# The sigmoid gates of two branches, made at the end of each RWKV group instead of in their branch projections

## The chip, the core and the metric

The kernel runs on one core of a Trainium2 chip. The metric is device time in microseconds (us) of one execution. Engines are named as the profile names them: PE is TensorE's matmuls and PEld its weight loads, DVE is VectorE, ACT is ScalarE, POOL is GpSimd, SP issues most of the DMAs.

## The reference

One layer of a hybrid decoder on 256 tokens of 2048 channels, in float32. One input projection feeds three mixers (Mamba-2 SSD, RWKV-7, mLSTM) and three sigmoid gates; each mixer's output is projected, gated, and the sum goes through an output projection, a layer norm and a gated MLP. What matters here is the end of the token mixer:

```
proj = h @ w_in
(ssd_z, ssd_xbc, ssd_dt, rwkv_p, ml_qk, ml_v, ml_o, ml_i, ml_f, gate_pre) = split(proj)
y_ssd, y_rwkv, y_mlstm = ssd_mixer(...), rwkv7_mixer(...), mlstm_mixer(...)
g_ssd, g_rwkv, g_mlstm = split(sigmoid(gate_pre), 3)
merged = g_ssd * (y_ssd @ proj_ssd) + g_rwkv * (y_rwkv @ proj_rwkv) + g_mlstm * (y_mlstm @ proj_mlstm)
return merged @ w_out
```

A gate depends on `h` alone, not on its mixer.

## The kernel before

**Products.** Each weight matrix is read in blocks of 512 columns, 256 rows (a chunk) at a time: SP loads the chunk (`wraw`, 512 KB, four buffers), ACT rounds it to the fast matmul format (`whi`, L154), DVE subtracts to get the low half (`wlo`, L155), and TensorE adds three products, high by high, high by low and low by high. A product over 2048 rows has 8 chunks. `block_cm` gives a block with the channels on the partitions (192 matmuls with 256 columns, L167, L169, L171), `block_tm` one with the tokens on the partitions (96 matmuls with 512 columns, L185 to L187). The accumulators `acc` have four banks of PSUM, two products' worth.

**Stages.** Four RWKV groups of eight heads (`rwkv_group`), four SSD groups, the branch projections of RWKV and SSD, the mLSTM (`ml_in`, eight heads), its branch projection, the output projection, and the MLP.

**An RWKV group.** Three products r, k, v (channel-major), then a gate product. Then a chain of small work: the decay and the rates from small matmuls (L476) with scans; normalised keys (L503, L514); pairwise products of four chunks of 64 tokens (L551) with masks; an inversion of triangular blocks, on VectorE four transposes (L586), 31 dependent steps shared by VectorE and GpSimd (L601, L603) and more transposes (L610, L613); the recursion over the four chunks (L645 to L679), in which each step waits for the one before; the output with its gate and a layer norm (L694 to L723), stored to `ydram`.

**Gates.** `gate(i, j, page)` (L892) makes columns 512 j to 512 j + 511 of gate i by a `block_tm` product and a sigmoid into a page of on-chip memory. In `rwkv_group` the gate of the RWKV branch (i = 1) is made behind r, k and v and stored to the DRAM tile `gdram` over ACT's DMA queue (L466, L467). In `branch` (L899) that gate is loaded back over SP's queue (L905), while the gates of SSD (i = 0) and mLSTM (i = 2) are made there, one ahead of each of the four projection products (L907). VectorE multiplies the gate with the projection and GpSimd adds it to `merged` (L914, L915).

**Order.** The code is written in the order above, and a list scheduler lays it out on each engine: of the instructions that are ready in its own model of time, the one that stands first in the code goes first; loads and splits of weights go ahead of all. The order is fixed when the program is built, and each engine then works its list from first to last. Products that stand behind a chain in the code therefore fill the places where the chain waits. Work slots (`p0` to `p18` and others) are shared by tag, so a tile also waits until the last reader of its slot is done.

Of the kernel before, what the change touches and what calls it, by code (L numbers as in the profile page):

```python
# [9 lines left out]
F32 = mybir.dt.float32  # L10
# [4 lines left out]
PSUM = bass.MemoryType.PSUM  # L15
DRAM = bass.MemoryType.DRAM

P = 128
T = 256
# [6 lines left out]
ALPHA = float(2.0 ** 0.25)  # L26
# [21 lines left out]
# pages that hold the last weights of a product whose token tiles end one after the other  # L48
LATE = [("b4", "p18"), ("b0", "b1"), ("b2", "b3"), ("p0", "p1"), ("p2", "p15"), ("p4", "p5")]

# columns of the one per-channel array: constants first, then vectors of the inputs
# [39 lines left out]
class Pair:  # L91
    """A channel-major operand split in two, as tiles of `n` row blocks each."""
# [11 lines left out]
class Layer:  # L104
# [11 lines left out]
    def pg(self, tag, shape, name, dtype=F32):  # L116
        """A tile in one of the shared work slots: p0..p17, b0..b4, s0..s3."""
        return self.wp.tile(shape, dtype, name=name, tag=tag)
# [14 lines left out]
    # ---------------------------------------------------------------- weights  # L133
    def chunks(self, W, nkt, pieces, pages=()):
        """hi and lo of row block after row block; the last chunks in the given pages."""
        nc, tc = self.nc, self.tc
        width = max(o + n for o, _, n in pieces)
        for c in range(0, nkt, KC):
            n = min(KC, nkt - c)
            self.nchunk += 1  # L140
            with tc.high_priority() if self.nchunk > 3 else nullcontext():
                raw = self.sp.tile([P, KC, 512], F32, name="wraw", bufs=4)
                for o, c0, w in pieces:
                    nc.sync.dma_start(
                        out=raw[:, :n, o:o + w],
                        in_=W[c * P:(c + n) * P, c0:c0 + w].rearrange("(k p) n -> p k n", p=P))
                i = c // KC - ((nkt + KC - 1) // KC - len(pages))
                if i < 0:
                    hi = self.sp.tile([P, KC, 512], F32R, name="whi")
                    lo = self.sp.tile([P, KC, 512], F32R, name="wlo", bufs=3)  # L150
                else:
                    hi, lo = [self.pg(t, [P, KC, 512], "wlate", F32R) for t in pages[i]]
                r = raw[:, :n, :width]
                nc.scalar.copy(out=hi[:, :n, :width], in_=r)  # L154
                nc.vector.tensor_tensor(out=lo[:, :n, :width], in0=r,  # L155
                                        in1=hi[:, :n, :width].bitcast(F32), op=ALU.subtract)
            for k in range(n):
                yield c + k, hi[:, k], lo[:, k]
# [19 lines left out]
    def block_tm(self, W, c0, X, nkt=KT, pages=()):  # L178
        """With pages the second token tile ends later, after all of the first."""
        nc = self.nc  # L180
        acc = [self.psA.tile([P, 512], F32, name="acc") for _ in range(2)]

        def mm(tt, kt, wh, wl):
            s = slice(tt * P, tt * P + P)
            nc.tensor.matmul(acc[tt], lhsT=X.h(kt)[:, s], rhs=wh, start=kt == 0, stop=False)  # L185
            nc.tensor.matmul(acc[tt], lhsT=X.h(kt)[:, s], rhs=wl, start=False, stop=False)  # L186
            nc.tensor.matmul(acc[tt], lhsT=X.l(kt)[:, s], rhs=wh, start=False, stop=kt == nkt - 1)  # L187

        late = []
        for kt, wh, wl in self.chunks(W, nkt, [(0, c0, 512)], pages):  # L190
            mm(0, kt, wh, wl)
            if kt // KC < (nkt + KC - 1) // KC - len(pages):
                mm(1, kt, wh, wl)
            else:
                late.append((kt, wh, wl))
        for w in late:
            mm(1, *w)
        return acc
# [6 lines left out]
    # ------------------------------------------------------------- layer norm  # L205
    def to_cm(self, n, gname, bname, X):
        """token-major normalised n -> X = g*n+b channel-major, split in two."""
        nc = self.nc
        hi, lo = X.hi[0], X.lo[0]
        for kt in range(0, KT, 2):  # L210
            ps = self.bank().rearrange("p (a t) -> p a t", a=2)
            for a in range(2):
                for tt in range(2):
                    c = (kt + a) % 4 * P
                    nc.tensor.transpose(out=ps[:, a, tt * P:(tt + 1) * P],  # L215
                                        in_=n(tt, (kt + a) // 4)[:, c:c + P], identity=self.c("ident"))
            tmp = self.pg("s%d" % (kt // 2 % 2), [P, 2, T], "tocm")
            for a in range(2):
                g, b = self.v(gname, kt + a), self.v(bname, kt + a)
                nc.scalar.activation(out=hi[:, kt + a], in_=ps[:, a], func=AF.Identity, scale=g, bias=b)  # L220
                nc.vector.tensor_scalar(out=tmp[:, a], in0=ps[:, a], scalar1=g, scalar2=b,
                                        op0=ALU.mult, op1=ALU.add)
            nc.vector.tensor_tensor(out=lo[:, kt:kt + 2], in0=tmp,
                                    in1=hi[:, kt:kt + 2].bitcast(F32), op=ALU.subtract)

    def moments(self, st, tt, act=False):
        """1/std, -mean/std and mean from the statistics of 4 column blocks."""
        nc, cp = self.nc, self.cp
        mv = cp.tile([P, 2], F32, name="mv", bufs=2)
        rstd = cp.tile([P, 1], F32, name="rstd", bufs=2)  # L230
# [15 lines left out]
    def normalise(self, blk, st):  # L246
        """blk(tt, j) <- (blk - mean) * rstd; one token tile on each of two engines."""
        nc = self.nc
        m = [self.moments(st, tt) for tt in range(2)]
        for j in range(NB):  # L250
            t = blk(0, j)
            nc.scalar.activation(out=t, in_=t, func=AF.Identity, scale=m[0][0], bias=m[0][1])
            t = blk(1, j)
            nc.vector.tensor_scalar(out=t, in0=t, scalar1=m[1][2], scalar2=m[1][0],
                                    op0=ALU.subtract, op1=ALU.mult)

    def affine_tm(self, r, name):
        """r <- r * g + b, token-major."""
        nc = self.nc
# [9 lines left out]
    def residual_tm(self, W, Y, nkt, r, st, before=None):  # L269
        """r <- ALPHA*r + Y^T W, with statistics per 512 columns."""  # L270
# [10 lines left out]
    # ---------------------------------------------------------------- evacuation  # L281
# [18 lines left out]
    # ---------------------------------------------------------------- prologue  # L300
    def prologue(self):
# [28 lines left out]
        # derived small vectors  # L330
# [7 lines left out]
    def smalls(self):  # L338
        """LoRA inputs, SSD time steps, mLSTM gates."""
# [16 lines left out]
        # softplus / log-sigmoid: i,f on partitions 64..79, dt on 96..127  # L356
# [22 lines left out]
        # q = atanh(s) = log1p(exp(-|x|)) / 2  # L379
# [8 lines left out]
        # SSD: local cumulative sums of a*dt  # L388
# [21 lines left out]
        # mLSTM: stabiliser  # L410
# [28 lines left out]
    # ---------------------------------------------------------------- RWKV-7  # L439
# [6 lines left out]
    def rwkv_group(self, g):  # L446
# [19 lines left out]
        gate = self.gate(1, g, 18)  # L466
        nc.scalar.dma_start(out=self.gdram[:, g], in_=gate)  # L467
# [12 lines left out]
        # decay: cumulative sums within chunks, then P and 1/P  # L480
# [16 lines left out]
        # normalised keys (negated)  # L497
# [20 lines left out]
        # kh = k (1 + (a-1) k_a)  # L518
# [5 lines left out]
        # av <- -(kk a)  # L524
        gps.tensor_tensor(out=av, in0=av, in1=nk, op=ALU.mult)
        # bonus
# [5 lines left out]
        # operands and pairwise products, chunk after chunk  # L532
# [30 lines left out]
        # token-major values  # L563
# [16 lines left out]
        # inverse of the unit triangular matrices: 32x32 diagonal blocks by substitution  # L580
# [54 lines left out]
        # chunks in order; rows: even heads R | Y, odd heads Y | R  # L635
# [44 lines left out]
        # output gate  # L680
# [16 lines left out]
        # per-head layer norm  # L697
# [27 lines left out]
    # ---------------------------------------------------------------- SSD  # L725
# [11 lines left out]
    def ssd_group(self, g, Y):  # L737
# [12 lines left out]
        # scores [s, l]: columns (s0,l0) (s0,l1) (s1,l1)  # L750
# [58 lines left out]
    # ---------------------------------------------------------------- mLSTM  # L809
# [34 lines left out]
    def ml_head(self, h, q, k, Y):  # L844
# [6 lines left out]
        # exponent: min(g[s] - c[l], mask)  # L851
# [39 lines left out]
    # ---------------------------------------------------------------- branches  # L891
# [6 lines left out]

    def branch(self, i, name, Y, merged, last=None):  # L899
        nc, a = self.nc, self.a  # L900
        vec, gps = nc.vector, nc.gpsimd
        for j in range(NB):
            if i == 1:
                g = self.pg("p%d" % (4 + j % 2), [P, 2, 512], "gate")
                nc.sync.dma_start(out=g, in_=self.gdram[:, j])  # L905
            else:
                g = self.gate(i, j, 4 + j % 2)  # L907
# [14 lines left out]
    def transposed(self, src, c0):  # L922
        """Two column tiles of token-major src(tt, c), channel-major in a PSUM bank."""
# [7 lines left out]
    def split_scaled(self, ps, w, hi, lo):  # L931
        """hi + lo = ps * w for one column tile in PSUM."""
# [8 lines left out]
    def run(self, upto=None):  # L941
# [3 lines left out]
        self.gdram = self.dp.tile([P, 4, 2, 512], F32, name="gdram")  # L945
# [100 lines left out]
def pack(i):  # L1046
    """Lays the inputs out for the kernel: weights as they are, per-channel vectors as columns."""
# [47 lines left out]
```

## Time and profile before

Three runs: 2489.68, 2487.14 and 2489.25 us, median 2489.25. The profiled execution has no time of its own beside its span of 2489.2 us, from the first to the last instruction, which lies between the runs.

| stretch of the span (us) | what runs | PE busy | DVE busy | POOL busy | granted clock |
|---|---|---|---|---|---|
| 0 to 118.7 | layer norm, first products | 101.7 | 80.0 | 5.6 | 1.00 |
| 118.7 to 773.4 | RWKV groups to the end of the last recursion | 606.0 | 567.1 | 333.7 | 0.97 |
| 773.4 to 902.5 | rest of SSD | 126.7 | 103.7 | 55.3 | 1.00 |
| 902.5 to 1173.3 | branches of RWKV and SSD, with 4 gates | 270.8 | 142.9 | 26.9 | 1.00 |
| 1173.3 to 1459.0 | mLSTM | 285.7 | 179.6 | 15.1 | 1.00 |
| 1459.0 to 1641.0 | branch of mLSTM, with 4 gates | 181.9 | 96.5 | 21.8 | 1.00 |
| 1641.0 to 1731.0 | output projection | 90.0 | 51.6 | 3.5 | 1.00 |
| 1731.0 to 2489.2 | layer norm, MLP, layer norm | 737.1 | 460.5 | 55.7 | 0.99, then 0.97 |

The columns are the time within the stretch in which the engine had an instruction under way, and the mean share of its clock that TensorE was granted. Matmuls overlap in their pipeline, so that PE can be busy without a gap and yet start matmuls at less than its full rate; the number of matmuls in a stretch shows that.

### The profile page before, as it was taken

The numbers are of one execution on the slowest core, as the hardware profiler recorded it, in microseconds if no ns is written. First come the engines' busy times: TensorE is split into PE (matmuls) and PEld (weight loads), VectorE is DVE, ScalarE is ACT, GpSimd is POOL, SyncE is SP. The second block draws the span as 40 slices with busy tenths as digits, with TensorE's granted clock in tenths as the row PEclk, the third lists the DMA queues.
The fourth block names the chain that finished last, engine by engine and source line by source line (L and its number), as shares of the span: only waits on it lengthen the run. The fifth ranks groups of instructions, "written<-read, shape, count | busy, mean of one in ns | idle before, by whom it ended". The sixth has DMA issues, their size and how long they took to land.

```text
span 2489.2 us, 41687 instructions
## 1 busy us (share of the span) xinstructions
PE 2399.9 (96%) x16602; PEld 2152.9 (86%) x16602; DVE 1681.8 (68%) x2116; ACT 1249.3 (50%) x1634; POOL 517.7 (21%) x488
## 2 busy tenths in 40 slices
PE   7999898989999999999999999999999999999997
PEld 7988787877989988888988888887999999997886
DVE  6678988897997875544666665456766666664445
ACT  4555455444646654443456654444554555453333
POOL 0046463564643520001000022000200000000000
PEclk9999999999999999999999999999999999999999
DMA  7654434244445656655655566555556556556554
GB/s 237 187 161 133 127 102 151 85 136 140 133 140 170 193 185 206 208 190 191 186 179 175 181 204 213 186 190 185 180 184 185 186 186 187 186 177 215 193 191 148
DMA packets 280276, 435.09 MB, mean 175 GB/s; under 512 B 25432, under 2 KB 118032, under 8 KB 279696
## 3 DMA queue, kind: packets, MB, share of 16 engines
q1 hardware_dynamic: 278640, 427.70, 54.4%
q8 instruction: 130, 2.13, 0.3%
q10 hardware_dynamic: 864, 2.62, 0.3%
q0 software_dynamic: 576, 2.10, 0.2%
q14 instruction: 66, 0.54, 0.1%
HBM read 423.90 MB, written 8.43 MB: 174 GB/s over the span
## 4 chain that ended last, share of the span: by engine, by line
PE 81%; DVE 11%; issue 3%; POOL 2%; ACT 2%; DMA 1%; SPq 0%; DVEq 0%; POOLq 0%; ACTq 0%
PE acc L186 13%; PE acc L187 13%; PE acc L185 13%; PE acc L171 12%; PE acc L169 12%; PE acc L167 12%; DVE wlo L155 4%; DVE si L603 1%; PE mix L551 1%; DVE si L601 1%; DVE xt L613 1%; DMA wraw<-in_w_in 1%; DVE ni L586 1%; ACT whi L154 1%; PE mix L788 1%
## 5 line engine op out<-in xcount | busy, mean ns | idle before, releaser
L155 DVE TENSOR_TENSOR wlo<-wraw,whi 128x1024 fp32r<-128x1024 f32 (+2 forms) x756 | 986.0, 1307 | 672.0 <-ACT whi L154 664.3
L154 ACT CAST whi<-wraw 128x1024 fp32r<-128x1024 f32 (+2 forms) x756 | 786.6, 1042 | 854.5 <-PE acc L187 446.0
L171 PE MATMUL acc<-xh,wlo 128*128 128x256 f32 x3104 | 887.2, 286 | 27.8 <-DVE wlo L155 27.5
L167 PE MATMUL acc<-xh,whi 128*128 128x256 f32 x3104 | 884.6, 285 | 3.0 <-ACT whi L154 2.7
L169 PE MATMUL acc<-xl,whi 128*128 128x256 f32 x3104 | 884.4, 285 | 0.0
L171 PEld LDWEIGHTS acc<-xh,wlo 128*128 128x128 f32 x3104 | 590.8, 191 | 36.8 <-DVE wlo L155 32.7
L167 PEld LDWEIGHTS acc<-xh,whi 128*128 128x128 f32 x3104 | 591.8, 191 | 8.2 <-ACT whi L154 3.1
L169 PEld LDWEIGHTS acc<-xl,whi 128*128 128x128 f32 x3104 | 591.1, 190 | 3.1 <-issue 1.0
L186 PE MATMUL acc<-wlo,xh 128*128 128x512 f32 x640 | 257.5, 402 | 9.2 <-DVE wlo L155 9.1
L187 PE MATMUL acc<-whi,xl 128*128 128x512 f32 x640 | 254.0, 397 | 0.0
L185 PE MATMUL acc<-whi,xh 128*128 128x512 f32 x640 | 233.9, 397 | 0.0
L186 PEld LDWEIGHTS acc<-wlo,xh 128*128 128x128 f32 x640 | 120.9, 189 | 38.7 <-DVE wlo L155 12.8
L185 PEld LDWEIGHTS acc<-whi,xh 128*128 128x128 f32 x640 | 120.9, 189 | 27.7
L187 PEld LDWEIGHTS acc<-whi,xl 128*128 128x128 f32 x640 | 121.0, 189 | 26.1
L186 PE MATMUL acc<-wlo,ah 128*128 128x512 f32 x322 | 126.9, 394 | 0.5 <-DVE wlo L155 0.5
L187 PE MATMUL acc<-whi,al 128*128 128x512 f32 x322 | 126.7, 393 | 0.0
L1006 POOL TENSOR_TENSOR fc<-fc 128x512 f32<-128x512 f32 (+1 forms) x22 | 28.7, 1303 | 447.2 <-DVE fc L293 440.3
L185 PE MATMUL acc<-whi,ah 128*128 128x512 f32 x322 | 113.4, 394 | 1.1 <-ACT whi L154 1.1
L915 POOL TENSOR_TENSOR merged<-merged,gate 128x512 f32<-128x512 f32 x16 | 28.2, 1788 | 342.8 <-DVE gate L914 342.8
L293 DVE SCALAR_TENSOR_TENSOR fc<-acc,fcols,fc 128x255 f32<-128x255 f32 (+1 forms) x172 | 77.0, 478 | 13.4 <-ACT fc L290 11.9
L266 POOL TENSOR_TENSOR res<-res,gb 128x1024 f32<-128x1024 f32 x16 | 43.7, 2730 | 203.3 <-PE mix L215 93.9
L603 POOL TENSOR_TENSOR yi<-yi,si 128x26 f32<-128x26 f32 (+12 forms) x104 | 73.3, 704 | 7.8
(360 smaller groups left out, 3134.2 us busy)
## 6 DMA issues: line engine op xcount, KB each, us to landing
wraw<-in_w_in SPq DMA_DIRECT2D x368, 512.0 KB, 3.4
wraw<-in_ffn_w_up SPq DMA_DIRECT2D x336, 256.0 KB, 3.1
wraw<-in_ffn_w_down SPq DMA_DIRECT2D x84, 512.0 KB, 4.4
wraw<-in_proj_rwkv SPq DMA_DIRECT2D x32, 512.0 KB, 4.5
wraw<-in_proj_ssd SPq DMA_DIRECT2D x32, 512.0 KB, 3.5
wraw<-in_proj_mlstm SPq DMA_DIRECT2D x32, 512.0 KB, 3.8
wraw<-in_w_out SPq DMA_DIRECT2D x32, 512.0 KB, 4.3
acb<-acd SPq DMA_DIRECT2D x16, 256.0 KB, 3.6
```

The costliest lines, as they stand in the source:

```text
L154: nc.scalar.copy(out=hi[:, :n, :width], in_=r)
L155: nc.vector.tensor_tensor(out=lo[:, :n, :width], in0=r, in1=hi[:, :n, :width].bitcast(F32), op=ALU.subtract)
L167: nc.tensor.matmul(a, lhsT=wh[:, o:o + m], rhs=X.h(kt), start=st, stop=False, skip_group_check=True)
L169: nc.tensor.matmul(a, lhsT=wh[:, o:o + m], rhs=X.l(kt), start=False, stop=False, skip_group_check=True)
L171: nc.tensor.matmul(a, lhsT=wl[:, o:o + m], rhs=X.h(kt), start=False, stop=kt == nkt - 1, skip_group_check=True)
L185: nc.tensor.matmul(acc[tt], lhsT=X.h(kt)[:, s], rhs=wh, start=kt == 0, stop=False)
L186: nc.tensor.matmul(acc[tt], lhsT=X.h(kt)[:, s], rhs=wl, start=False, stop=False)
L187: nc.tensor.matmul(acc[tt], lhsT=X.l(kt)[:, s], rhs=wh, start=False, stop=kt == nkt - 1)
L266: nc.gpsimd.tensor_tensor(out=r[j], in0=r[j], in1=gb[:, i].unsqueeze(1).to_broadcast([P, 2, 512]), op=op)
L293: nc.vector.scalar_tensor_tensor(out=dst[:, j:], in0=ps[:, :T - j], scalar=v(wname, (width - 1 - j) * nch + ct), in1=dst[:, j:], op0=ALU.m ...
L603: eng.tensor_tensor(out=t[:, j + 1:32, lo:e], in0=t[:, j + 1:32, lo:e], in1=tv, op=ALU.subtract)
L1006: nc.gpsimd.tensor_tensor(out=u, in0=u, in1=t[1][:, :n], op=ALU.mult)
```

## The change

The gates of SSD and mLSTM are made at the end of each RWKV group, behind its output in the code: for group g, block g of gate 0 and block g of gate 2, each stored to `gdram`, which grows from four to twelve blocks. `branch` loads every gate. The page p18 takes all of them in turn. The number of products, sigmoids and bytes of weights is the same; there are eight more stores and eight more loads of 512 KB. Comments are gone, which shifts some lines.

```
 (rwkv_group, behind v)
-        gate = self.gate(1, g, 18)
-        nc.scalar.dma_start(out=self.gdram[:, g], in_=gate)
+        self.spill_gate(1, g)
...
 (rwkv_group, end)
         nc.gpsimd.dma_start(out=self.ydram[:, 4 * g:4 * g + 4], in_=yo)

+        for i in (0, 2):
+            self.spill_gate(i, g)
...
+    def spill_gate(self, i, j):
+        self.nc.scalar.dma_start(out=self.gdram[:, i, j], in_=self.gate(i, j, 18))
+
     def branch(self, i, name, Y, merged, last=None):
         nc, a = self.nc, self.a
         vec, gps = nc.vector, nc.gpsimd
         for j in range(NB):
-            if i == 1:
-                g = self.pg("p%d" % (4 + j % 2), [P, 2, 512], "gate")
-                nc.sync.dma_start(out=g, in_=self.gdram[:, j])
-            else:
-                g = self.gate(i, j, 4 + j % 2)
+            g = self.pg("p%d" % (4 + j % 2), [P, 2, 512], "gate")
+            nc.sync.dma_start(out=g, in_=self.gdram[:, i, j])
             acc = self.block_tm(a[name], 512 * j, Y)
...
-        self.gdram = self.dp.tile([P, 4, 2, 512], F32, name="gdram")
+        self.gdram = self.dp.tile([P, 3, 4, 2, 512], F32, name="gdram")
```

The scheduler lays the whole RWKV stage out anew. The first place is VectorE in the recursion of group 1. `zm`, `zve` and `zvo` are the recursion's state; `nr`, `nrr`, `kh`, `nk`, `sq`, `l1e`, `l1o` and `bk` belong to the preparation and the pairwise products of group 2; `wlo` is the low half of a chunk of weights. Before:

```order
L155 TENSOR_TENSOR wlo<-wraw,whi 128x1024
L506 TENSOR_SCALAR nr<-nr 128x256
L669 COPY zm<-seq 128x256
L507 RECIPROCAL nr<-nr 128x256
L671 TENSOR_TENSOR zve<-zm,pl 64x4x64
L671 TENSOR_TENSOR zvo<-zm,pl 64x4x64
L155 TENSOR_TENSOR wlo<-wraw,whi 128x1024
L203 TENSOR_TENSOR nrr<-nr,nrr 128x256
L521 TENSOR_SCALAR kh<-av,cst,oka 128x256 x4
L155 TENSOR_TENSOR wlo<-wraw,whi 128x1024
L544 TENSOR_TENSOR l1e<-r,pext 64x4x64
L544 TENSOR_TENSOR l1o<-r,pext 64x4x64
```

The same place of the changed kernel (its lines L666, L668 and L670 are L667, L669 and L671 before; `v` is the evacuation of group 2's product v):

```order
L668 COPY zm<-seq 128x256
L670 TENSOR_TENSOR zve<-zm,pl 64x4x64
L670 TENSOR_TENSOR zvo<-zm,pl 64x4x64
L155 TENSOR_TENSOR wlo<-wraw,whi 128x1024 x2
L285 SCALAR_TENSOR_TENSOR v<-acc,cst,v 128x255
L155 TENSOR_TENSOR wlo<-wraw,whi 128x1024
L285 SCALAR_TENSOR_TENSOR v<-acc,cst,v 128x255 x2
L666 TENSOR_TENSOR zm<-zm,seq 128x256
L285 SCALAR_TENSOR_TENSOR v<-acc,cst,v 128x255
L670 TENSOR_TENSOR zve<-zm,pl 64x4x64
L670 TENSOR_TENSOR zvo<-zm,pl 64x4x64
L155 TENSOR_TENSOR wlo<-wraw,whi 128x1024 x5
```

Before, the preparation of group 2 stood between the steps of group 1's recursion; now weight splits and evacuations of products stand there, and the preparation comes behind the recursion.

The second place is TensorE where the mLSTM ends and its branch begins. `mn` is the output of the last head, transposed by L927 (L929 of the changed kernel), `acc_14479` the first gate of the branch, `acc_14628` its first projection product. Before:

```order
L927 MATMUL mix_14462<-cst_72,mn_14432 128x128
L185 MATMUL acc_14479<-whi_14609,xh_73 128x512
L186 MATMUL acc_14479<-wlo_14610,xh_73 128x512
L187 MATMUL acc_14479<-whi_14609,xl_74 128x512
L185 MATMUL acc_14480<-whi_14609,xh_73 128x512
L186 MATMUL acc_14480<-wlo_14610,xh_73 128x512
L187 MATMUL acc_14480<-whi_14609,xl_74 128x512
L185 MATMUL acc_14628<-whi_14632,ymh_11803 128x512
L185 MATMUL acc_14629<-whi_14632,ymh_11803 128x512
```

Now, where `acc_15093` and `acc_15094` are the first projection product and `acc_15259` and `acc_15260` the second; `ymh_12415` and `ymh_12416` are the first and the second half of the mLSTM's output:

```order
L929 MATMUL mix_15074<-cst_72,mn_15044 128x128 x3
L185 MATMUL acc_15259<-whi_15281,ymh_12415 128x512
L185 MATMUL acc_15260<-whi_15281,ymh_12415 128x512
...
L185 MATMUL acc_15259<-whi_15299,ymh_12415 128x512
L185 MATMUL acc_15260<-whi_15299,ymh_12415 128x512
L185 MATMUL acc_15093<-whi_15223,ymh_12416 128x512
L186 MATMUL acc_15093<-wlo_15224,ymh_12416 128x512
L185 MATMUL acc_15094<-whi_15223,ymh_12416 128x512
```

Before, a gate product filled the time up to the last transposes; now the first projection product is broken off ahead of its last chunk (`whi_15223`), which needs the last head, and the second one is drawn ahead.

## The prediction

> **What bounds the kernel now.** I read the page first (busy tenths over 40 slices, then the chain that ended last), then the busy time by stage, then the waits inside one RWKV group.
>
> ```profile
> PE   7999898989999999999999999999999999999997
> ...
> DVE  6678988897997875544666665456766666664445
> ...
> PE 81%; DVE 11%; issue 3%; POOL 2%; ACT 2%; DMA 1%; SPq 0%; DVEq 0%; POOLq 0%; ACTq 0%
> ```
>
> TensorE (PE) carries the chain; VectorE (DVE) has its 11% where its tenths reach 8 and 9, in slices 3 to 13, the RWKV groups. A slice is 62 us.
>
> ```profile
> core 0: us, PE busy (x) PEld busy (x) DVE busy (x) ACT busy (x) POOL busy (x), PEclk, DMA share, GB/s
> 425.80:581.50 155.70, 140.94 (x1304) 125.11 (x1296) 136.16 (x185) 80.14 (x126) 83.91 (x97) 0.98 0.39 123
> 1000.00:1050.00 50.00, 50.00 (x219) 40.78 (x218) 25.02 (x26) 23.54 (x25) 3.53 (x2) 1.00 0.62 205
> 1850.00:1900.00 50.00, 50.00 (x424) 50.00 (x423) 30.79 (x36) 24.46 (x30) 2.59 (x2) 1.00 0.61 184
> ```
>
> The last two rows give the price of a product at full rate. In the branch stage 219 matmuls of 128x512 start in 50 us, 0.228 us each, so a token-major product of 96 costs 21.9 us. In the FFN stage 424 of 128x256 start in 50 us, 0.118 us each, so a channel-major one of 192 costs 22.6 us. The first row is one RWKV group: it holds three channel-major products and one gate, 89.7 us at these prices, and takes 155.7 us.
>
> ```profile
> PEld acc L171 <- DVE wlo L155: 12.0, 5, 5.0
> ...
> PE acc L171 <- DVE wlo L155: 11.0, 5, 4.8
> DVE wlo L155 <- ACT whi L154: 9.6, 5, 3.2
> ```
>
> These are waits of the group before it (268 to 426 us): when TensorE waits in a product it is for the low half of the weights, which VectorE makes between its other work. So a gate made in the branch stage costs its full 21.9 us, while in a group there is time in which TensorE starts nothing. The question is how much of that time two more products can use.
>
> **The change part by part.** *Removed from the branches*: eight gate products, 8 x 21.9 = 175 us of a stage that runs at full rate. *Added to the groups*: the same eight, two per group. To see what they cost there I cut a group's period at two marks: the start of its last pairwise product (L551) and of its first recursion product (L645). Rows by group:
>
> ```profile
> L551 PE MATMUL mix<-l1e,bk x32: 272/272/373, 177.4 to 202.4; 64*128 64x128 f32 x32
> L551 PE MATMUL mix<-l1o,bk x32: 272/272/418, 178.2 to 205.5; 64*128 64x128 f32 x32
> ...
> L551 PE MATMUL mix<-l1o,bk x32: 272/272/373, 303.9 to 334.8; 64*128 64x128 f32 x32
> ...
> L551 PE MATMUL mix<-l1o,bk x32: 272/272/373, 458.3 to 487.4; 64*128 64x128 f32 x32
> ...
> L551 PE MATMUL mix<-l1o,bk x32: 272/272/579, 616.4 to 645.8; 64*128 64x128 f32 x32
> ...
> L645 PE MATMUL seq<-zve,l1e x32: 222/222/270, 270.0 to 324.0; 128*64 128x64 f32 x32
> ...
> L645 PE MATMUL seq<-zve,l1e x32: 222/222/270, 412.6 to 466.0; 128*64 128x64 f32 x32
> ...
> L645 PE MATMUL seq<-zve,l1e x32: 222/222/270, 557.2 to 611.7; 128*64 128x64 f32 x32
> ```
>
> From mark to mark the three periods are 129.3, 152.6 and 158.4 us (205.5 to 334.8 and so on), 440.3 together. Each falls into the inversion (205.5 to 270.0: 64.5; then 77.8 and 69.8) and the rest (270.0 to 334.8: 64.8; then 74.8 and 88.6). Counting the product matmuls that the order puts into each stretch, at the two prices:
> - inversion: 47.2, 51.7, 48.1 us before, 47.8 in every group now;
> - rest: 30.0, 36.3, 45.1 us before, 85.9 now.
>
> So what is not product was 17.3, 26.1 and 21.7 us in the inversion, and 34.8, 38.5 and 43.5 in the rest. A period now holds 47.8 + 85.9 = 133.7 us of products.
>
> What a period may cost follows from the ends. Up to the last pairwise product of group 0 the order now has 162.9 us of products, before 155.7: that mark moves to 205.5 + 7.2 = 212.7. Up to that of group 3 it has 564.0, before 414.1, so 149.9 us less is left to do behind it. With a period C the time saved is 645.8 + 149.9 - 212.7 - 3C = **3 x (194.3 - C)**.
>
> *The inversion.* VectorE sets it (substitution steps, transposes and 15 weight splits, the same now). I take 64.5 from group 0, the only row in which no output of an earlier group stands in this stretch, as none does now, plus 0.6 for products: 65.1. The upper end is group 1's 77.8.
>
> *The rest.* The recursion, the preparation of the next group and its pairwise products lay on top of each other; in the new order the preparation comes behind the recursion, with more products between. The trace shows no such stretch, so from both sides. Lower end: only the small matmuls stay.
>
> ```profile
> 279.23 0.61 PE seq L651 x16
> ...
> 303.00 2.03 PE mix L551 x15
> ```
>
> These pieces of the chain give 0.038 us for a recursion-like matmul and 0.135 for a pairwise one. Of the 632 small ones in a group (1304 less 672) 432 are of the first sort: 16 + 27 = 43 us a period at most, or 26 in the rest when 17 belong to the inversion. So 85.9 + 26 = 112. Upper end: the three parts one behind the other, each as slow as where they overlapped.
>
> ```profile
> L676 PE MATMUL seq<-zvo,bp x32: 218/218/267, 284.8 to 332.1; 64*64 64x64 f32 x32
> ...
> L476 PE MATMUL mix<-alo__757,lw x8: 377/378/380, 139.9 to 141.9; 96*128 96x256 f32 x8
> ```
>
> Recursion of group 0: 270.0 to 332.1, 62.1, with 30.0 of products; now 40.2, so 72.3. Preparation of group 0: 141.9 to 177.4 (the first pairwise product, l1e), 35.5 with 29.7; now 26.0, so 31.8. Pairwise: 28.1 with 15.8; now 19.7, so 32.0. Together 136.1. I take the remainder of group 0, 34.8, the row with the least foreign work, which gives 85.9 + 34.8 = 120.7: more products per step of the recursion cover more of its latency, and VectorE no longer does pairwise work in it.
>
> C = 65.1 + 120.7 = 185.8, and the saving is 3 x 8.5 = 25.5 us.
>
> *VectorE in the groups.* Each gate brings 8 weight splits.
>
> ```profile
> L155 DVE TENSOR_TENSOR wlo<-wraw,whi 128x1024 fp32r<-128x1024 f32 x131 | 184.0, 1412 | 30.0 <-ACT whi L154 29.5
> ...
> L155 DVE TENSOR_TENSOR wlo<-wraw,whi x15: 1224/1226/1227, 1599.9 to 1639.4; 128x1024 fp32r<-128x1024 f32 x15
> ```
>
> 16 x 1.41 = 22.6 us a period on top of 136.2 make 158.8, under C by 27, and none of the added splits falls into the inversion; I cost them at nothing, hidden by the products in the rest. Without that cover each is 1.4 us. The second row, from 1600 to 1640 us where GpSimd does nothing, has 1.226 us, so in the groups a split is 0.19 us longer on average. [...]
>
> *Sigmoids, stores and loads.*
>
> ```profile
> L896 ACT ACTIVATE gate<-acc x24: 587/598/602, 144.4 to 1620.2; 128x512 f32<-128x512 f32 x24
> ...
> DMA to landing us min/median/max: 3.2/5.1/6.3
> ```
>
> All 24 sigmoids stay; 16 move, 2.4 us of ScalarE (ACT) a period, beside products. A store lands in at most 6.3 us while the next gate, in the same page p18, ends a product later. The eight loads go out on SP ahead of their products as the four do now; nothing, or at 5.1 us each 41 us if none were ahead.
>
> *The end of mLSTM.* The first gate of its branch covered the last head; now that branch's own product does.
>
> ```profile
> L927 PE MATMUL mix<-cst,mn x8: 270/272/328, 1463.9 to 1485.8; 128*128 128x128 f32 x8
> ...
> L934 DVE SCALAR_TENSOR_TENSOR yml<-mix,cst,ymh x4: 475/478/485, 1469.7 to 1489.5; 128x256 fp32r<-128x256 f32 x4
> ```
>
> The last block of Y is ready 4.2 us behind its transposes (1485.8 to 1490.0). The order now has 14 product matmuls there, 3.2 us, then other products between; the wait is 0 to 4 us, I take 2.
>
> Sum: against the profiled span of 2489.2 us, which is the median of the runs (2489.25) within 0.1 us: 2489.2 - 25.5 + 2 = **2466 us**.
>
> **Rivals.**
> 1. *The products fill everything and TensorE alone sets the period.* For it: VectorE has 27 us to spare. Against: it is full in the inversion, which stays. C = 133.7 + 43 = 176.7 gives 2438; with 34, midway between 24 (all 632 at 0.038) and 43, C is 168 and the time 2412. The clock belongs here.
>
> ```profile
> 267.60:425.80 158.20, 142.05 (x1384) 127.83 (x1376) 142.22 (x184) 78.82 (x127) 85.86 (x95) 0.96 0.38 120
> ...
> 581.50:740.00 158.50, 146.93 (x1430) 136.82 (x1427) 143.78 (x219) 86.77 (x130) 85.05 (x94) 0.96 0.43 135
> ```
>
> The granted clock is 0.96 to 0.98 in the groups and 1.00 in the branches; closed gaps would return 2 to 4% of some 156 us, 3 to 6 us a period. [...] I don't take it, since the inversion's gaps remain. Chance 0.18.
> 2. *Nothing is absorbed.* The remainder stays as it was on average (60.6), C is 194.3, the time 2491. Speaks for it: the instructions of the chain are the same, each as late as before. Chance 0.13.
> 3. *Slower: the preparation behind the recursion lengthens the chain of a group.* At the upper end of the rest C is 65.1 + 136.1 = 201.2, and the time 2489.2 + 20.7 + 2 = 2512. It decides from C = 194.3 on, a rest of 129.2. For it: the order itself, in which the next preparation stands behind the recursion. Against: its parts ran slow because they overlapped. Chance 0.22.
>
> That the gates are not made in the groups is excluded: the order has all twelve stores there.
>
> **How the numbers follow.** The forecast case, C from 178 to 192, is 2443 to 2484 and has 0.47. What a measurement can tell from no change is about 0.2%, 5 us: faster is the forecast and rival 1 (0.65), the same is rival 2 (0.13), slower rival 3 (0.22). The range 2430 to 2500 leaves out the far halves of rivals 1 and 3.
>
> **What the profile after would show.** The last pairwise products at 213, 398, 584 and 770 us and the first recursion products 65 behind each. Products of the branches 22 us each without a gate between, from the first to the last; a hole at the start of the mLSTM branch over 4 us, or a load of a gate awaited, refutes those terms. A rest over 129 us with TensorE waiting in L645 or L503 would make rival 3 right, a rest under 112 rival 1.

## The result, and the profile after

| | us, median | lowest to highest | runs |
|---|---|---|---|
| before | 2488.22 | 2487.14 to 2489.68 | 4 |
| after | 2508.55 | 2505.99 to 2511.75 | 4 |

The ratio is 1.0081, with a 95% interval of [1.0068, 1.0093]: the changed kernel is 0.8% slower. The profiled execution after has a span of 2504.2 us, before 2489.2.

The page of the changed kernel, busy tenths in slices of 62.6 us and the chain that ended last by engine:

```profile
PE   7999998899898999999999999999999999999997
...
DVE  6778677766956978875556666655866666665545
...
PE 73%; DVE 13%; POOL 5%; issue 3%; DMA 3%; ACT 2%; SPq 0%; DVEq 0%; ACTq 0%; POOLq 0%
```

Beside TensorE and VectorE the chain now has 5% of GpSimd (POOL) and 3% of DMAs, where it had 2 and 1. Where the time went, the marks of the prediction show: the last pairwise product of each group (L550, L551 before) and the first product of each recursion (L644, L645 before). Columns are count, shortest, median and longest ns, first and last start:

```profile
L550 PE MATMUL mix<-l1o,bk x32: 272/272/373, 179.5 to 207.3; 64*128 64x128 f32 x32
L550 PE MATMUL mix<-l1o,bk x32: 272/272/578, 372.9 to 411.1; 64*128 64x128 f32 x32
L550 PE MATMUL mix<-l1o,bk x32: 272/272/578, 576.8 to 612.9; 64*128 64x128 f32 x32
L550 PE MATMUL mix<-l1o,bk x32: 272/272/578, 779.0 to 816.9; 64*128 64x128 f32 x32
...
L644 PE MATMUL seq<-zve,l1e x32: 222/222/270, 273.0 to 324.8; 128*64 128x64 f32 x32
L644 PE MATMUL seq<-zve,l1e x32: 222/222/270, 475.4 to 527.6; 128*64 128x64 f32 x32
L644 PE MATMUL seq<-zve,l1e x32: 222/222/270, 677.2 to 730.9; 128*64 128x64 f32 x32
```

The periods are 203.8, 201.8 and 204.0 us (forecast 185.8): inversions of 65.7, 64.3 and 64.3 (forecast 65.1), rests of 138.1, 137.5 and 139.7 (forecast 120.7). The whole loss is in the rests.

The busy times of the stretch from the first of these marks to the last, before:

```profile
core 0: us, PE busy (x) PEld busy (x) DVE busy (x) ACT busy (x) POOL busy (x), PEclk, DMA share, GB/s
205.50:645.80 440.30, 402.72 (x3694) 359.72 (x3693) 392.15 (x544) 229.46 (x360) 234.84 (x276) 0.97 0.39 123
```

And the same stretch of the changed kernel:

```profile
207.30:816.90 609.60, 560.92 (x4371) 486.55 (x4369) 435.48 (x586) 289.73 (x424) 244.66 (x280) 0.94 0.48 140
```

It is 169.3 us longer. By the instruction order it holds 400.9 us of products where it held 258.2 (at the prediction's prices), 142.7 more. The other 26.6 are two things. TensorE stands idle for 48.7 us (609.6 less 560.9) where it was idle for 37.6: 11.1 more. And its busy time beyond the products is 160.0 where it was 144.5: 15.5 more, with a granted clock of 0.94 where it was 0.97. So no idle time was filled. The row of the kernel before shows how little there was: 37.6 us in three periods.

What TensorE waits for in that stretch now, in the changed kernel (total us, times, longest):

```profile
PE acc L171 <- DVE wlo L155: 19.1, 27, 3.3
PE mix L550 <- ACT bk L559: 17.3, 3, 6.6
PE seq L714 <- DVE yt L708: 8.7, 3, 2.9
PE seq L620 <- DVE x L609: 3.6, 6, 0.7
```

The second and the third are not among TensorE's waits before, and each comes once in a period. The third is for the layer norm ahead of the transposes of a group's output. The second is for a small copy by ScalarE (ACT). What ScalarE did then is in its timeline (start, us, line, operation, and in brackets the idle time before it with what ended it):

```profile
584.77 0.59 ACT L559 COPY bk<-mix 128x512 f32<-128x512 f32 x1 [0.33 <-PE mix L558]
...
587.90 1.05 ACT L154 CAST whi<-wraw 128x1024 fp32r<-128x1024 f32 x1 [0.59 <-PE acc L187]
599.42 0.62 ACT L202 CAST gx<-glo__758 128x512 fp32r<-128x512 f32 x1 [10.47 <-DMA ydram<-yo]
600.06 0.59 ACT L559 COPY bk<-mix 128x512 f32<-128x512 f32 x1
```

and in that of GpSimd, of the same time:

```profile
580.82 2.41 POOL L720 TENSOR_TENSOR yo<-yo,v 128x1024 f32<-128x1024 f32 x1
...
586.82 2.40 POOL L721 TENSOR_TENSOR yo<-yo,gg 128x1024 f32<-128x1024 f32 x1
...
592.37 0.59 POOL L722 DMA_DIRECT2D ydram<-yo  x1
```

The wait of ScalarE for that store in the whole stretch, before and now:

```profile
ACT gx L202 <- DMA ydram<-yo: 11.1, 1, 11.1
...
ACT gx L202 <- DMA ydram<-yo: 33.1, 3, 11.6
```

`gx`, an operand of a group's output gate, depends on an early result alone, and the scheduler puts it early. But it lies in page p14, as `yo` does, the output of the group before. So it waits until the store of `yo` has landed, 7 us behind its issue at 592.4; and the output comes late now, in the middle of the next group's pairwise products. ScalarE starts nothing else meanwhile: the casts of weights and the copies of `bk` that stand behind `gx` in its list wait with it for 10.5 us, and TensorE waits for `bk`, 4.8 us in this period. Before, that wait came once, in an inversion (it ended at 384.1 us).

The branches did as the prediction had it. Two stretches of the changed kernel, the SSD branch and the end of the mLSTM with the start of its branch:

```profile
1192.80:1280.00 87.20, 87.20 (x387) 72.17 (x386) 46.36 (x47) 35.88 (x35) 10.60 (x6) 1.00 0.68 223
...
1500.00:1600.00 100.00, 100.00 (x462) 82.26 (x461) 63.54 (x94) 57.80 (x91) 16.38 (x6) 1.00 0.68 217
```

Four products of 96 matmuls start in 87.2 us, 21.8 each, and no gate between them; at the end of the mLSTM TensorE has no idle time.

### The profile page after: what moved, and what is told of

It is laid out like the page before. It is cut to its first block, busy times and chain, and to the rows that moved or that the text cites. A ratio compares the mean times of both kernels' runs of the same rounds, so it can differ in the third digit from the quotient of the medians.

```text
span 2504.2 us, 41710 instructions
## 1 busy us (share of the span) xinstructions
PE 2407.5 (96%) x16602; PEld 2152.9 (86%) x16602; DVE 1665.7 (67%) x2116; ACT 1240.6 (50%) x1627; POOL 521.3 (21%) x488
## 4 chain that ended last, share of the span: by engine, by line
PE 73%; DVE 13%; POOL 5%; issue 3%; DMA 3%; ACT 2%; SPq 0%; DVEq 0%; ACTq 0%; POOLq 0%
PE acc L171 12%; PE acc L169 11%; PE acc L167 11%; PE acc L187 11%; PE acc L186 11%; PE acc L185 11%; DVE wlo L155 4%; DVE si L600 1%; DVE si L602 1%; POOL bk L544 1%; DMA ydram<-yo 1%; DMA wraw<-in_ffn_w_down 1%; ACT whi L154 1%; DVE ni L585 1%; POOL l1e L542 1%
## 5 line engine op out<-in xcount | busy, mean ns | idle before, releaser
L155 DVE TENSOR_TENSOR wlo<-wraw,whi 128x1024 fp32r<-128x1024 f32 (+2 forms) x756 | 997.9, 1323 | 698.8 <-ACT whi L154 693.3
L171 PE MATMUL acc<-xh,wlo 128*128 128x256 f32 x3104 | 889.7, 287 | 28.9 <-DVE wlo L155 28.9
L169 PEld LDWEIGHTS acc<-xl,whi 128*128 128x128 f32 x3104 | 593.1, 191 | 2.3 <-issue 0.7
L185 PE MATMUL acc<-whi,xh 128*128 128x512 f32 x640 | 242.5, 401 | 0.0
L266 POOL TENSOR_TENSOR res<-res,gb 128x1024 f32<-128x1024 f32 x16 | 43.5, 2716 | 202.7 <-DMA res<-ntm 91.8
L600 POOL TENSOR_TENSOR si<-yi,ni 128x26 f32<-128x26 f32 (+12 forms) x104 | 79.5, 764 | 18.6 <-DVE ni L585 10.7
L186 PEld LDWEIGHTS acc<-wlo,ah 128*128 128x128 f32 x322 | 60.4, 188 | 14.8 <-DVE wlo L155 1.5
```

Of the source, the lines that this page charges most:

```text
L155: nc.vector.tensor_tensor(out=lo[:, :n, :width], in0=r, in1=hi[:, :n, :width].bitcast(F32), op=ALU.subtract)
L169: nc.tensor.matmul(a, lhsT=wh[:, o:o + m], rhs=X.l(kt), start=False, stop=False, skip_group_check=True)
L171: nc.tensor.matmul(a, lhsT=wl[:, o:o + m], rhs=X.h(kt), start=False, stop=kt == nkt - 1, skip_group_check=True)
L266: nc.gpsimd.tensor_tensor(out=r[j], in0=r[j], in1=gb[:, i].unsqueeze(1).to_broadcast([P, 2, 512]), op=op)
L600: eng.tensor_tensor(out=tv, in0=t[:, j:j + 1, lo:e].to_broadcast(sh), in1=N[:, j + 1:32, j:j + 1].to_broadcast(sh), op=ALU.mult)
```

## The experiments

Two theories of the loss stood at first. A: the wait of ScalarE for the store of `yo`. B: the order, in which the preparation of the next group comes behind the recursion instead of within it. Diffs are against the changed kernel unless they say otherwise. The kernel before ran beside each; its medians were 2487.86 (e1 to e4), 2488.71 (e5 to e8) and 2487.55 us (e9, e10).

**e1: `yo` in page p12 instead of p14.**

```
-        yo = self.p4(14, "yo")
+        yo = self.p4(12, "yo")
```

> The changed kernel with the output tile yo in page p12 instead of p14. In its profile the split of gx of the next group (ACT) waits 10.5 us for the store of yo, since both use p14, and ACT's weight casts stand behind it while the pairwise products run. Theory A (that wait on ACT makes the rest of a period long): the pairwise stretch of groups 1 to 3 falls from 36 to 39 us to the 28 us of group 0, the period from 203 to 193 us, and the time by 3 x 10 = 30 us to 2478 us. Theory B (the preparation behind the recursion makes the chain long, whatever ACT does): the time stays within 5 us of 2508 us.

2487.85 us (2483.60 to 2491.15, 11 runs), ratio to before 1.0001 [0.9992, 1.0010]. The order of TensorE's products is that of the changed kernel. p12 is not `yo`'s alone (`gw`, `ni` and `x1` of a group use it too), but no cast of `gx` waits in e1. Its stretch from first to last mark:

```profile
208.90:793.40 584.50, 550.07 (x4370) 476.33 (x4369) 439.85 (x583) 288.13 (x421) 249.55 (x280) 0.97 0.49 145
```

TensorE's waits in it:

```profile
PE acc L171 <- DVE wlo L155: 19.2, 27, 3.0
PE seq L714 <- DVE yt L708: 11.5, 3, 3.9
PE seq L620 <- DVE x L609: 3.7, 6, 0.7
```

The wait for `bk` is gone, and the stretch is 25.1 us shorter: 14.3 of idle time, 10.9 of busy time. The second part goes with a lower granted clock behind the wait (0.54 from 600.0 to 606.0 us). The pairwise products of group 2 and what lies among them, in the changed kernel (group 2's recursion and preparation above them):

```profile
475.40:538.60 63.20, 60.19 (x557) 49.72 (x556) 33.20 (x45) 33.21 (x56) 5.25 (x7) 0.97 0.51 149
538.60:576.30 37.70, 34.81 (x165) 27.67 (x159) 30.48 (x40) 21.17 (x29) 19.07 (x17) 0.91 0.48 139
576.30:612.90 36.60, 31.81 (x189) 27.59 (x189) 19.20 (x17) 14.94 (x21) 22.68 (x18) 0.91 0.51 159
```

and in e1:

```profile
470.40:530.60 60.20, 58.67 (x558) 48.18 (x556) 31.74 (x43) 32.13 (x53) 4.00 (x7) 1.00 0.54 156
530.60:569.00 38.40, 34.56 (x164) 27.52 (x160) 31.28 (x39) 21.64 (x30) 20.68 (x18) 0.91 0.48 137
569.00:598.70 29.70, 29.70 (x190) 25.59 (x189) 20.13 (x18) 14.61 (x20) 22.73 (x17) 1.00 0.60 193
```

The last rows hold the same work: 36.6 us at a clock of 0.91 against 29.7 without an idle moment at 1.00. So theory A carries 21 us of the time, the whole loss against the kernel before; but A had expected a gain of ten, which did not come. Eight gates in the groups then cost what they cost in the branches.

**e2: the same edit in the kernel before.**

> The kernel before with the same page for yo. There the split of gx waits 11.1 us too, but in the inversion, which VectorE fills. Theory A: 0 to 10 us a group are to be had, so 2460 to 2488 us. Theory B: within 5 us of 2488 us.

2495.54 us (2490.88 to 2500.40, 6 runs), ratio 1.0030 [1.0019, 1.0042]. The kernel before has that wait once, for 11.1 us, and e2 is no faster without it. The edit lays the order out anew there (inversions of 97 to 103 us in groups 1 to 3, rests of 60), so it is no clean test; it says only that the page is no gain by itself.

**e3: all three gates behind v, ahead of the group's chain.**

```
-        self.spill_gate(1, g)
+        for i in (1, 0, 2):
+            self.spill_gate(i, g)
...
-        for i in (0, 2):
-            self.spill_gate(i, g)
```

> The changed kernel with all three gates of a group behind its product v in the code, ahead of the chain of small work, none at its end. r, k and v of the next group then fill the chain again as before. Theory B: the preparation of the next group lies beside the recursion again, the period falls from 203 to between 171 (six products and the small matmuls at full rate) and 190 us, the time to between 2412 and 2476 us. Theory A: it depends only on where the split of gx stands; if it still waits while products are due, 2500 to 2515 us.

2486.74 us (2483.19 to 2493.50, 11 runs), ratio 0.9996 [0.9987, 1.0005]. Periods are 223.6, 168.9 and 224.5 us. The preparation is not brought into the recursion evenly: the normalised keys of group 1 begin 24.8 us behind the end of the recursion (351.0 to 375.8), those of group 2 3 us ahead of its start. Neither theory's time came: it lies above B's range and below A's. The test of B was spoilt by its own side effect.

**e4: one gate alone, that of SSD; the gate of mLSTM is made in its branch again.**

```
-        for i in (0, 2):
+        for i in (0,):
             self.spill_gate(i, g)
...
+            if i < 2:
                 (load the gate)
+            else:
+                g = self.gate(i, j, 4 + j % 2)
```

> The changed kernel with gate 0 alone at the end of each group, gate 2 in its branch as before. If each moved gate costs the same, 2498 us. Theory B: with five products a period the chain is as long (about 200 us less what is hidden), so the period is 190 to 203 us, the products taken from the branches only 88 us, and the time over 2508 us. Theory A: the wait of ACT is paid as often, 2500 to 2530 us.

2479.10 us (2475.63 to 2481.73, 5 runs), ratio 0.9963 [0.9950, 0.9975]: faster than both kernels and below all three expectations, so the effect is not proportional to the number of gates. Of ScalarE's wait for the store 1.5 us are left in the stretch. Rests are 94.4, 111.0 and 109.2 us and hold 49.6, 66.9 and 64.1 us of products: 44.8, 44.1 and 45.1 beyond them, as in e1 (45.2, 42.4 and 44.5 beyond 85.9), although the preparation here begins within the recursion. That gave theory F against B: what a rest takes beyond its products does not depend on the place of the preparation. S, below, is B with its number.

**e5: no gates of SSD and mLSTM.**

```
-        for i in (0, 2):
-            self.spill_gate(i, g)
...
-            nc.sync.dma_start(out=g, in_=self.gdram[:, i, j])
+            nc.sync.dma_start(out=g, in_=self.gdram[:, 1, j])
```

> Leaves out the gates of SSD and mLSTM: those branches multiply with the gate of RWKV, loaded from DRAM. It closes the account: what eight gates cost where they are made. Theory F (TensorE had next to nothing free in the groups: a stretch costs its products plus a remainder that does not shrink): the RWKV groups are as before, and the branches lose 8 products of 21.9 us and what stood beside them, so 2305 to 2313 us; eight gates then cost 22 to 23 us each in the branches, about the same in the groups of run e1, and over 24 in the changed kernel. Theory S (the groups have room, and it is lost to the serial preparation): the same time here, since nothing moves; a time under 2295 or over 2320 would say that a gate's price in the branches was misread.

2317.99 us (2316.81 to 2319.90, 4 runs), ratio 0.9315 [0.9302, 0.9328]: 5 us over what I expected. A gate in a branch costs 170.7 / 8 = 21.3 us. This is the yardstick of the table below. The order in its groups is that of the kernel before, and so its stretch from the first mark to the last shows how far two executions of one order differ:

```profile
205.90:645.70 439.80, 411.65 (x3695) 368.06 (x3693) 390.64 (x545) 229.28 (x360) 234.72 (x276) 0.94 0.42 123
```

It is as long as that before (440.3), with a clock of 0.94 for 0.97 and 28.2 us of idle time for 37.6. So a lower mean clock is not by itself a longer stretch. The rest of group 0 has 30.3 us beyond its products here, where it had 34.8.

**e6: e4 with `yo` in p12.**

> Run e4 with yo in a page of its own; the scheduler then puts the whole preparation of groups 2 and 3 at the start of the recursion, and 15 us of products later than in e4. Rests hold 49.6, 38.3 and 38.3 us of products, inversions 51.5, 64.8 and 73.4. Theory F (remainder of a rest 44.6 wherever the preparation stands, of an inversion 16.7): rests 94, 83, 83, inversions 68, 81, 90, and 2474 to 2484 us, as e4. Theory S (a preparation inside the recursion gives the remainder of 34.8 that I had forecast): rests 84, 73, 73 and 2440 to 2460 us.

2473.44 us (2470.36 to 2476.88, 5 runs), ratio 0.9939 [0.9927, 0.9952]. The time is F's within a microsecond; the rests are not. They are 92.8, 71.8 and 72.8 us with 49.6, 38.3 and 38.3 of products: 43.2 beyond them in the first, but 33.5 and 34.5 in the others. What sets these apart is where the normalised keys of the next group (L502) begin. In e6, before the recursion:

```profile
L502 PE MATMUL mix<-sq,cst x8: 378/392/406, 446.5 to 446.8; 128*32 128x256 f32 x8
...
L644 PE MATMUL seq<-zve,l1e x32: 221/222/271, 448.2 to 510.1; 128*64 128x64 f32 x32
```

In the kernel before (line L503), ahead of the first recursion at 270.0, and behind the start of the second at 412.6:

```profile
L503 PE MATMUL mix<-sq,cst x8: 379/391/404, 267.3 to 267.6; 128*32 128x256 f32 x8
...
L503 PE MATMUL mix<-sq,cst x8: 379/391/405, 425.4 to 425.7; 128*32 128x256 f32 x8
```

So the 34.8 us that the prediction took over from group 0 belongs to a rest that does not hold the first part of the preparation: it was done in the inversion. The rests that hold it have 38.5 and 43.5 in the same kernel. But a second thing differs in these rows: the transposes of the group's output. They start behind the mark that ends the rest in group 0 of the kernel before (354.2; mark 334.8) and in the last two periods of e6 (532.5 and 702.6; marks 520.0 and 689.6), so those rests do not hold them either. Neither F nor S was right as it stood.

**e7: both gates between the preparation and the pairwise products of their group.**

```
+        for i in (0, 2):
+            self.spill_gate(i, g)
         L1, BK, BP, ZV = self.L1, self.BK, self.BP, self.ZV
...
-        for i in (0, 2):
-            self.spill_gate(i, g)
```

> Both gates stand in the code between the preparation and the pairwise products of their group, not behind its output. The normalised keys of the next group then come 25.8 us of products into the rest, within the recursion (39.0 in the changed kernel, at its end); inversions hold 52.7 us of products, rests 80.9. Theory F (TensorE is full, remainders stay 16.7 and 44.6): inversion 69, rest 125 to 133 (the upper end if ScalarE still waits for the page of yo), period 195 to 202, 2487 to 2511 us. Theory S (the serial preparation is the cause): rest 116, period 185, 2455 to 2470 us.

2478.97 us (2476.89 to 2481.47, 5 runs), ratio 0.9961 [0.9949, 0.9974]: all eight gates in the groups, and yet 30 us below the changed kernel. It lies between F and S. Its stretch:

```profile
216.60:793.00 576.40, 548.91 (x4373) 474.64 (x4371) 445.25 (x594) 300.24 (x436) 251.18 (x281) 0.98 0.50 149
```

With the same 401 us of products TensorE is idle for 27.5 us, its clock is 0.98, and periods are 190.4, 188.7 and 197.3. The wait ahead of the output's transposes is gone as well.

**e8: e7 with `yo` in p12.**

> Run e7 with yo in a page of its own, the same order of products. Theory F: rest 125, period 195, 2484 to 2494 us, whatever e7 gives. Theory S: rest 116, period 185, 2455 to 2470 us. If e7 and e8 differ by about 20 us, the wait of ScalarE for the store of yo is there in e7 as in the changed kernel.

2477.92 us (2475.51 to 2479.28, 5 runs), ratio 0.9955 [0.9941, 0.9968], the same as e7. In e7 5.5 us of ScalarE's wait are left, of 33.1 in the changed kernel, with the page still shared: the long wait comes with the late output of the changed order, not with the shared page alone.

**e9: one gate (SSD) at the place of e7, `yo` in p12. e10: the RWKV gate there too.**

```
-        self.spill_gate(1, g)          (e10 only)
...
+        for i in (0,):                 (e10: (1, 0))
+            self.spill_gate(i, g)
         L1, BK, BP, ZV = self.L1, self.BK, self.BP, self.ZV
```

> One moved gate (that of SSD), between preparation and pairwise products, yo in a page of its own, the gate of mLSTM in its branch. Rests hold 49.6, 45.0 and 46.8 us of products, inversions 51.5, 64.8 and 66.7. If a time follows from how much of TensorE's waiting in the groups is filled, and the place of the preparation matters only through that, it lies by e4 and e6: 2470 to 2480 us. If a preparation that is spread over the recursion is what pays (it starts with the recursion in groups 2 and 3 here as in e6), 2465 to 2474, as e6 or below.

> Run e9 with the gate of RWKV moved from behind v to the same place: the preparation no longer stands behind a gate product in the code. The first pairwise products come 9 us of products earlier; rests 60.5, 55.2 and 50.5 us of products, inversions 52.2, 54.0 and 59.2. If waiting is filled as in e9, 2468 to 2478 us; if TensorE has nothing more to fill, as e9 within 5 us.

e9: 2471.40 us (2470.36 to 2477.31, 5 runs), ratio 0.9945 [0.9931, 0.9958]; e10: 2474.47 us (2473.06 to 2475.82, 5 runs), ratio 0.9948 [0.9935, 0.9960]. Both are as e6, within what the runs can tell apart, and both times lie in both of their expected ranges, so neither run decides between the two readings it was made for. In e9 the rests beyond their products are 41.8, 35.8 and 37.3; in the last two the keys come 2 us ahead of the recursion, and the output's transposes 2 us behind the mark.

**All of them in one table**: the profiled executions, from the first mark to the last. Beyond products is the length of the stretch less its products, so idle time and other busy time together. The last column is what a moved gate costs, from the medians: time less e5, less 21.3 us for each gate still made in a branch, by the number of moved gates.

| | stretch | products | PE idle | beyond products | clock | us per moved gate |
|---|---|---|---|---|---|---|
| before | 440.3 | 258.2 | 37.6 | 182.1 | 0.97 | (21.3) |
| after | 609.6 | 400.9 | 48.7 | 208.7 | 0.94 | 23.8 |
| e1 | 584.5 | 400.9 | 34.4 | 183.6 | 0.97 | 21.2 |
| e2 | 442.0 | 271.7 | 28.1 | 170.3 | 0.96 | |
| e3 | 617.1 | 432.6 | 28.9 | 184.5 | 0.96 | 21.1 |
| e4 | 515.0 | 331.2 | 32.1 | 183.8 | 0.96 | 18.9 |
| e5 | 439.8 | 258.2 | 28.2 | 181.6 | 0.94 | |
| e6 | 483.3 | 316.0 | 33.9 | 167.3 | 0.98 | 17.5 |
| e7 | 576.4 | 401.1 | 27.5 | 175.3 | 0.98 | 20.1 |
| e8 | 575.4 | 401.0 | 27.7 | 174.4 | 0.98 | 20.0 |
| e9 | 492.9 | 324.5 | 30.0 | 168.4 | 0.97 | 17.0 |
| e10 | 507.0 | 331.7 | 31.2 | 175.3 | 0.97 | 17.8 |

The forecast needed 156.5 (557.4 less 400.9) in the column beyond products. No order reached it.

## Why the prediction was wrong

The forecast was 2466 us, the profiled span after 2504.2: 38.6 us more than the sum before its rounding (2465.6). By its own cut: the first mark came at 207.3 instead of 212.7 (-5.4); three periods took 609.6 us instead of 557.4 (+52.2); what follows the last mark took 1687.3 instead of 1843.4 - 149.9 + 2 = 1695.5 (-8.2).

- *What bounds the kernel, the products' prices, the gates leaving the branches*: right. Behind the last mark 156.1 us went away, 8.2 more than forecast; where these came from was not found.
- *The inversion* (65.1): right within 0.8 us in each group.
- *The rest* (120.7): **the step that failed is the remainder of 34.8 us taken from group 0**. It measured 52.2, 51.6 and 53.8. Some 9 us of it are left without ScalarE's wait: e1, with the same order, has 44 on average, and the 27 us by which its stretch exceeds the forecast are this. The row taken over did not hold the work that the new rests hold. The first part of the preparation lay in the inversion there, and so did the transposes of the output and half of the matmuls of its gate. By the starts of the matmuls, e1's rests have 2.2 us more of preparation, 2.5 more of output, 2.0 more of idle time (3.8 in each stand ahead of the output's transposes) and 2.9 more in large products that start further apart. I had chosen this row as the one with the least foreign work, in the same section that put the preparation behind the recursion and found no output in the inversion any more.
- *What is open in it*: how much the place of the preparation does alone. The rests with 33 to 37 in e6 and e9 lack both its first part and the output's transposes. One rest parts the two: in e3's second (101.4 us, 34.6 beyond products) the keys lie ahead of the recursion and the transposes (588.1 to 593.1; mark 608.1) within. That speaks for the preparation, but it is one rest, and two executions of one order differ by as much as 4.5 us in a rest (34.8 before, 30.3 in e5).
- *What no step had*: ScalarE's wait for the page of `yo`, 25 us of the stretch by e1, 14.3 of it TensorE's idle time; the other 10.9 go with a lower clock behind the wait. The prediction looked at the page that the gates share (p18) and at their stores, not at what a later output does to the other pages. The row of that wait stood in the profile of the kernel before, once, in an inversion.
- *The reason given* ("more products per step of the recursion cover more of its latency"): wrong in kind. It counted as latency what is mostly TensorE's own small work: of 182.1 us beyond products before, 37.6 were idle, some 32 went into large products that start further apart than their price, and 112 into small matmuls. The row quoted there said so: 155.70 us, PE busy 140.94.
- *VectorE at nothing*: right as far as its load goes; 435 of 609.6 us busy. A split took 1.40 us on average in the stretch before and after, so a higher price of a split did not come.
- *Loads of gates, the end of the mLSTM*: right; TensorE has no wait for a load in the row of the SSD branch nor in that of the mLSTM's end (busy 87.20 of 87.20 us and 100.00 of 100.00), and the term of 2 us was not seen as idle time.
- *The clock*: rival 1 had it rise as gaps close. It fell, 0.97 to 0.94, with more idle time (48.7 us for 37.6), and stood at 0.97 to 0.98 in e1, e6, e7 and e9. That new gaps alone did this is not shown: e5 has 0.94 in the order of before, with less idle time (28.2 us).
- *Rivals*: rival 3 (2512) came out in sign, size and place, but its parts differ, and that its sum is so near is in part luck. Recursions took 62.8 to 64.7 us (it had 72.3), the preparation about 37 (31.8), and the pairwise products 36 to 39 (32.0) because of a wait that it did not know; without that wait they take 29.7. Its decisive point, a rest of 129.2, was right: e1 with 129.9 on average runs in the time of before, which is what rival 2 gives at a period of 194.3 (e1: 194.8).

In e6 and e9 the rests take 7 to 10 us less beyond their products where the preparation begins ahead of the recursion, and the whole stretches 15 to 17 us less beyond products than those of e1 and e4. In e6 most of that comes back behind the last mark, where the last output's transposes now lie too: e6 and e4 make the same gates in the groups, e6's stretch is 31.7 us shorter (15.2 of it products), and what follows is 27.9 us longer (1785.5 for 1757.6). Of the medians 5.7 us are left, with e9 7.7. And in e2 the keys come ahead of the recursion in all three periods (30.3, 32.1 and 34.9 beyond products), and it is not faster. So more than these 6 to 8 us is not shown for any such order. In e7 the preparation begins within the recursion, and a period is 2.7 us below that of e1 on average, where theory S had 10. But e7 also has more products in the inversion (52.7 for 47.8 us); which of the two brings its gain was not separated, and why e2 is slower was not found.

## What to carry to other kernels

Before idle time of an engine is counted as room, take its busy time out of the stretch: what is left beyond the large operations can be the engine's own small work, here 112 of 182.1 us, and that goes where the work goes. A remainder taken over from one group as a term is good only if the same work lies in it as in the new order. And where a reordering makes an output later, look for every tile that shares its slot: here ScalarE stood still for 33.1 us, in three waits of one early tile for a late store, with all that was queued behind it, which cost 21 us and went away with one page number.

## What was unexpected of the hardware

The granted clock was low behind a short wait: in the changed kernel TensorE waits 2.89 us for the layer norm ahead of its transposes, and the products behind that wait start 0.43 us apart instead of 0.23. Its timeline:

```profile
558.62 1.08 PE L714 MATMUL seq<-cst,yt 128*128 128x128 f32 x4 [2.89 <-DVE yt L708]
...
562.07 0.63 PE L187 MATMUL acc<-whi,xl 128*128 128x512 f32 x1
562.49 0.63 PE L185 MATMUL acc<-whi,xh 128*128 128x512 f32 x1
562.92 0.63 PE L186 MATMUL acc<-wlo,xh 128*128 128x512 f32 x1
```

The granted clock in that place:

```profile
559.50:565.80 6.30, 6.30 (x21) 4.93 (x21) 5.34 (x5) 2.19 (x4) 5.27 (x3) 0.60 0.59 166
```

It is 0.60 in the mean of these 6.3 us, and TensorE counts as busy all the time, with 21 matmuls. The same wait in the other two periods, 2.89 and 2.88 us, has 0.67 in the 5 us behind it; one of 2.21 us in the kernel before (up to 347.5) has 1.00 in the 4.5 us behind it. But the clock was also low with hardly a wait. In e1, behind 64 matmuls of 32x32 (L620) and 1.2 us of waiting, the full-size products of the next 4.8 us run at a granted clock of 0.50 (their starts 0.21 us apart, elsewhere 0.118):

```profile
458.00:463.00 5.00, 3.79 (x71) 3.41 (x70) 4.91 (x4) 1.26 (x2) 0.00 (x0) 0.84 0.38 108
463.00:467.80 4.80, 4.80 (x24) 4.80 (x24) 4.76 (x3) 2.82 (x4) 0.00 (x0) 0.50 0.00 0
```

Whether it is the small size of these matmuls that lowers the clock was not tried.
